# A two-layer hybrid decoder on one core: other layouts for the stored queries and keys, a norm vector moved into weights, and reordered work at the stage borders

## Chip, core and metric

The kernel runs on one core of a Trainium2 chip. The metric is the device time of one execution in microseconds (us). TensorE multiplies matrices and also does the transposes; VectorE (DVE), ScalarE (ACT) and GpSimd (POOL) work on tiles; SyncE (SP) issues nearly all DMAs here, and 16 DMA engines carry them out.

## The reference, cut to what matters

```python
D_MODEL, SEQ, DEPTH = 1024, 1024, 2       # 8 heads of 64 of either kind, 32 experts of width 256
def rms_norm(x, gain):
    return x * rsqrt(mean(x * x, -1) + 1e-6) * gain

def hybrid_mixer(xn, ...):                # xn = rms_norm(h, attn_norm[l])
    fq, fk, fv, f_logit, c_q, c_kv, k_rope = split(xn @ w_in)
    fox = attention(fq, fk, fv, decay=cumsum(log_sigmoid(f_logit + b_f)))
    q  = rms_norm(c_q, q_norm) @ w_uq     # 64 plain + 32 rotary columns per head
    kv = rms_norm(c_kv, kv_norm) @ w_ukv  # 64 key + 64 value columns per head
    mla = attention(rotary(q), [k_nope, rotary(k_rope)], v)
    return concat(norm(fox), norm(mla)) @ w_o

def reference(x, ...):
    h = x
    for l in range(DEPTH):
        h = h + hybrid_mixer(rms_norm(h, attn_norm[l]), ...)
        h = h + hierarchical_moe(rms_norm(h, ffn_norm[l]), ...)   # top 1 group, top 2 experts in it
    return rms_norm(h, final_norm)
```

All inputs and the output are float32.

## The kernel before, in words

Every product is made of split operands: `split` (L181 to L188) writes a rounded high part on ScalarE (L184, L187) and the rest on DVE (L185, L188), and `mm3` (L190 to L196) makes three TensorE passes of them. `split` takes a scale per partition if one is given.

A layer runs through these stages, each written out as straight code for 8 blocks of 128 tokens:

1. *Norm and first projection* (`chain_a`, `chain_b`, `transposes`, `misc_mm`, L405 to L486). For each block: in layer 1 the two expert rows y are added to h (`chain_c`); ScalarE squares and sums (L412); GpSimd takes the rsqrt in six small steps (`mean_rsqrt`, `rsqrt`, L163 to L179); DVE multiplies the row by its rsqrt and by the vector `attn_norm`, which a DMA has spread over all 128 partitions (`gb`, L417); TensorE transposes the block in eight pieces (L426), whose copies are split into xT; and `misc_mm` multiplies it with the 424 columns of w_in that hold the forget logits and the latents. The weights of these columns come in 8 pieces (`wa_piece`). In the loop at L475 block i+1 is transposed ahead of the projection of block i.
2. *Projections* (L745 to L797). Six chunks of 256 columns of w_in: v twice, (q, 0), (q, 1), (k, 0), (k, 1). The weights of the next chunk are loaded and split while a chunk runs (`prepare`: per chunk four pieces of two row blocks, 512 columns in all). A q or k chunk has four steps, each with one product of 24 passes; `take` splits the result into a staging tile `st` and stores it in HBM: FQ holds per head the high part twice and the low part once, FK the low and the high part, and both hold four more rows per head for ones and for the decay (`forget_d`). Each step then runs a few jobs of a list: first 18 jobs for decay, latents and rotary keys, then 12 for V, and from `late_pools` on (at (k, 0)) loads of w_uq and w_ukv and the upward projections: rotary and plain queries (MQR, MQ) and plain keys (MK).
3. *Hand-over* (L799 to L839). `load_ops` reads the four operand tiles of head 0 back from FQ and FK, the last FK result is taken, 8 value products follow, and `load_ops` of head 1. The operand buffers `op` lie where the second half of xT was.
4. *Attention*, 16 heads with two operand buffers (`load_ops` again, one head ahead), and the output projection with the router.
5. *Experts*, 32 per layer; the weights stream in. A loop for crowded experts follows (L1614), which ran no round in the profiled execution.

Behind the second layer the last stage (L1648 to L1668) adds the two expert rows to each block (`combined`, L225), takes the norm and stores the block; the output of a block is made behind the next block's sum.

TensorE, ScalarE, DVE and GpSimd execute in the order written. The order of SP's DMAs is chosen by a planner when the kernel is built: among the DMAs that its model holds to be ready, the one written first. Each engine runs its queue in order, so an instruction that waits holds up all behind it.

## Time and profile before

| | |
|---|---|
| median of 3 runs | 1942.1 us (1937.24 to 1949.56) |
| the profiled execution: time, span | 1941.36 us, 1939.6 us |
| TensorE busy, mean granted clock | 90% of the span, 0.959 |
| DVE, ScalarE, GpSimd busy | 70%, 61%, 30% |
| HBM read, written | 347.24 MB, 94.37 MB |
| layer 0: norm and first projection, projections, attention and output, experts | about 0 to 60, 60 to 238, 238 to 620, 620 to 932 us |
| layer 1, the same | about 932 to 1010, 1010 to 1182, 1182 to 1560, 1560 to 1875 us |
| last stage | 1875 to 1939.6 us |

Shares are of the span of one profiled execution. The granted clock is TensorE's: 1.0 is 2.4 GHz, 0.5 is 1.2 GHz. A busy engine need not be the bound, and an idle one costs only where the work that ends last waits for it.

### The profile page before, as it was taken

The numbers are of one execution on the slowest core, as the hardware profiler recorded it, in microseconds if no ns is written. First come the engines' busy times: TensorE is split into PE (matmuls) and PEld (weight loads), VectorE is DVE, ScalarE is ACT, GpSimd is POOL, SyncE is SP. The second block draws the span as 40 slices with busy tenths as digits, with TensorE's granted clock in tenths as the row PEclk, the third lists the DMA queues.
The fourth block names the chain that finished last, engine by engine and source line by source line (L and its number), as shares of the span: only waits on it lengthen the run. The fifth ranks groups of instructions, "written<-read, shape, count | busy, mean of one in ns | idle before, by whom it ended". The sixth has DMA issues, their size and how long they took to land.

```text
span 1939.6 us, 33742 instructions
## 1 busy us (share of the span) xinstructions
PE 1742.0 (90%) x12509; PEld 1410.5 (73%) x12509; DVE 1362.6 (70%) x2180; ACT 1184.9 (61%) x2254; POOL 587.2 (30%) x849
## 2 busy tenths in 40 slices
PE   7999899999996999999499997999999979999960
PEld 6987678888785777666399876888878757776640
DVE  6463478888336999888565345888863689998855
ACT  4442378888312898878344334888861268888751
POOL 4001145233313334332331021532241243343315
PEclk9999989999997999999799998999999979999995
DMA  5247833453763999999742776344547479999986
GB/s 162 66 114 213 274 134 111 101 121 88 248 210 135 359 357 353 362 353 357 273 156 53 185 242 219 110 121 107 119 144 251 153 268 365 350 347 358 351 298 221
DMA packets 145380, 427.11 MB, mean 220 GB/s; under 512 B 22166, under 2 KB 37564, under 8 KB 142140
## 3 DMA queue, kind: packets, MB, share of 16 engines
q1 hardware_dynamic: 129788, 387.14, 60.5%
q0 software_dynamic: 14336, 33.58, 5.2%
q10 hardware_dynamic: 1088, 4.19, 0.6%
q8 instruction: 100, 1.64, 0.4%
q14 instruction: 68, 0.56, 0.1%
HBM read 347.24 MB, written 94.37 MB: 228 GB/s over the span
## 4 chain that ended last, share of the span: by engine, by line
PE 60%; DMA 24%; DVE 6%; ACT 6%; issue 2%; POOL 1%; SPq 1%; POOLq 0%; ACTq 0%; DVEq 0%
PE ps L194 9%; PE ps L195 9%; PE ps L196 9%; DMA gu<-in_w_gate_dram 8%; PE S L873 8%; DMA gu<-in_w_up_dram 6%; PE pt L902 6%; DMA dn<-in_w_down_dram 6%; PE y L916 3%; PE gu L195 2%; PE gu L196 2%; PE gu L194 2%; ACT pr L894 2%; PE y L1140 1%; DVE nm L885 1%
## 5 line engine op out<-in xcount | busy, mean ns | idle before, releaser
L1482 DVE TENSOR_TENSOR lo<-gu,hi 128x1024 fp32r<-128x1024 f32 x248 | 298.0, 1221 | 42.1 <-ACT hi L1481 41.3
L1481 ACT ACTIVATE hi<-gu 128x1024 fp32r<-128x1024 f32 x248 | 257.9, 1059 | 29.7 <-DMA gu<-in_w_up_dram 21.1
L873 PE MATMUL S<-op 96*128 96x512 f32 (+3 forms) x960 | 228.8, 372 | 18.2 <-DMA op<-FK 11.6
L885 DVE TENSOR_REDUCE nm<-S 128x1 f32<-128x1024 f32 (+7 forms) x256 | 183.1, 752 | 67.2 <-PE S L877 67.2
L195 PE MATMUL gu<-lo,V 128*96 128x512 f32 x512 | 206.0, 402 | 11.9 <-DVE lo L1482 11.5
L894 ACT ACTIVATE pr<-S,nm 128x1024 f32<-128x1024 f32 (+7 forms) x256 | 189.2, 755 | 36.3 <-DVE nm L885 36.1
L194 PE MATMUL gu<-hi,V 128*96 128x512 f32 x512 | 206.8, 404 | 1.2 <-ACT hi L1481 0.6
L196 PE MATMUL gu<-hi,V 128*96 128x512 f32 x512 | 204.0, 399 | 0.9 <-DVE V L185 0.3
L904 ACT ACTIVATE ph<-pt 128x512 f16<-128x512 f32 x288 | 157.3, 601 | 66.6 <-PE pt L902 65.7
L1531 POOL DMA_INDIRECT y<-V,sidx x64 | 81.9, 1280 | 372.8 <-ACT V L1530 359.2
L905 DVE SCALAR_TENSOR_TENSOR pl<-pt,ph 128x512 f16<-128x512 f32 x288 | 184.7, 682 | 8.9 <-ACT ph L904 7.8
L873 PEld LDWEIGHTS S<-op 96*128 96x128 f32 (+1 forms) x960 | 161.3, 196 | 35.7 <-DMA wor<-in_w_o_dram 6.9
L1482 DVE TENSOR_TENSOR lo<-dn,hi 128x1024 fp32r<-128x1024 f32 x128 | 156.1, 1221 | 18.4 <-ACT hi L1481 14.8
L902 PE MATMUL pt<-ident,pr 128*128 128x128 f32 x1152 | 155.2, 278 | 8.6 <-DVE pl L905 3.5
L1481 ACT ACTIVATE hi<-dn 128x1024 fp32r<-128x1024 f32 x128 | 135.0, 1056 | 21.5 <-DMA dn<-in_w_down_dram 21.3
L902 PEld LDWEIGHTS pt<-ident,pr 128*128 128x128 f32 x1152 | 125.4, 143 | 13.9 <-ACT pr L894 13.0
L195 PEld LDWEIGHTS gu<-lo,V 128*96 128x96 f32 x512 | 83.5, 163 | 58.6 <-DVE lo L1482 29.0
L916 PE MATMUL y<-V,ph 128*128 128x64 f16 x2304 | 121.6, 193 | 2.8 <-ACT ph L904 1.6
L916 PEld LDWEIGHTS <-ph 128*128 128x128 f16 x2304 | 116.9, 98 | 5.3 <-ACT ph L904 1.8
L916 PE MATMUL y<-V,pl 128*128 128x64 f16 x1152 | 117.0, 193 | 1.1 <-DVE pl L905 1.0
L196 PEld LDWEIGHTS gu<-hi,V 128*96 128x96 f32 x512 | 83.4, 163 | 38.3 <-DVE V L185 6.2
L175 POOL TENSOR_SCALAR rs_v<-ss 128x1 f32<-128x1 f32 (+1 forms) x44 | 20.6, 468 | 289.6 <-ACT xn L1096 150.5
(363 smaller groups left out, 4366.0 us busy)
## 6 DMA issues: line engine op xcount, KB each, us to landing
gu<-in_w_gate_dram SPq DMA_DIRECT2D x124, 512.0 KB
gu<-in_w_up_dram SPq DMA_DIRECT2D x124, 512.0 KB
dn<-in_w_down_dram SPq DMA_DIRECT2D x60, 1024.0 KB
raw<-in_w_in_dram SPq DMA_DIRECT2D x48, 256.0 KB
h<-ht SPq DMA_DIRECT2D x17, 512.0 KB
FQ<-st SPq DMA_DIRECT2D x32, 256.0 KB
FK<-st SPq DMA_DIRECT2D x32, 256.0 KB
MQ<-st SPq DMA_DIRECT2D x16, 512.0 KB
```

The costliest lines, as they stand in the source:

```text
L194: pe.matmul(ps, sh(kc), mh(kc), start=first and i == 0, stop=False)
L195: pe.matmul(ps, sh(kc), ml(kc), start=False, stop=False)
L196: pe.matmul(ps, sl(kc), mh(kc), start=False, stop=last and i == n - 1)
L873: pe.matmul(o, a[0:k, qs], b[0:k, c0:c0 + n], start=bank not in started, stop=pi == len(passes) - 1 and not diag, skip_group_check=True)
L885: dve.tensor_reduce(nm, u["S"][:, col:col + (qb + 1) * P], axis=AX.X, op=OP.max, negate=True)
L894: act.activation(u["pr"][:, s], u["S"][:, s], AF.Exp, bias=nm, accum_out=zst[h // 2][:, qb, h % 2:h % 2 + 1])
L902: pe.transpose(pt[:, b], u["pr"][:, (4 * q + b) * P:(4 * q + b + 1) * P], ident)
L904: act.activation(u["ph"][:, ks], pt, AF.Copy, scale=P_SCALE)
L905: dve.scalar_tensor_tensor(u["pl"][:, ks], pt, P_SCALE, u["ph"][:, ks], op0=OP.mult, op1=OP.subtract)
L916: pe.matmul(yst[h][:, qb], a[:, b], v[:, kb, h % H, c], start=first_y[h], stop=(kb == qb and s == 2), skip_group_check=True)
L1481: act.activation(h_, raw, AF.Copy)
L1482: eng.tensor_tensor(l_, raw, h_.bitcast(F32), op=OP.subtract)
```

## The change

- FQ and FK are stored in the layout [head x 64 rows, 2 parts, tokens], with the rows for ones and decay in small tensors of their own (FQC, FKC). A result of 128 rows (two heads) goes out in one DMA. `load_ops` reads six pieces in place of four: each part into partitions 0 to 63, the part that is needed twice a second time into partitions 64 to 127, and the four extra rows.
- `late_pools` stands one chunk earlier, at (q, 1); every step runs 3 jobs (4 before in the k chunks). Four of the eight MK products are taken out of the list and made between the first four value products of the hand-over, behind the loads of head 0.
- `attn_norm` is no longer spread over the partitions. Its 16 rows are loaded once, transposed on TensorE into the columns `ga`, and the splits of the w_in pieces take their column as scale. Pieces of two row blocks are therefore split in two halves of 256 columns. The rows of h are scaled on ScalarE.
- The first projection stands in front of the transposes of block 1; its copy out of PSUM (`misc_take`) stands where it was.
- The block h[7] is loaded into a second staging tile; the tile `ht` is gone.
- Last stage: the sixteen y loads get sixteen tiles and are written ahead of the load of `final_norm`; the output of a block is made behind the sum of the block after next.

The diff, without the lines that only hand over a parameter or a tile:

```diff
+    arow = const.tile([DEPTH * KC, P], F32, name="arow")
+    sp.dma_start(arow, attn_norm.rearrange("l (c p) -> (l c) p", p=P))
+    ga = const.tile([P, DEPTH * KC], F32, name="ga")
...
-        gb = stg.tile([P, D], F32, name="st")
-        hx.append(stg.tile([P, D], F32, name="st"))
+        hx += [stg.tile([P, D], F32, name="st") for _ in range(2)]
...
-                    bcast_row(gb, attn_norm[l])
...
-        FQ = dram.tile([H, 3 * HD + 4, T], F32R, name=f"FQ{l}")
-        FK = dram.tile([H, 2 * HD + 4, T], F32R, name=f"FK{l}")
+        FQ = dram.tile([H * HD, 2, T], F32R, name=f"FQ{l}")
+        FK = dram.tile([H * HD, 2, T], F32R, name=f"FK{l}")
+        FQC = dram.tile([H, 4, T], F32R, name=f"FQC{l}")
+        FKC = dram.tile([H, 4, T], F32R, name=f"FKC{l}")
...
-            split(wah[k], wal[k], wraw[k])
+            split(wah[k], wal[k], wraw[k], ga[:, l * KC + k:l * KC + k + 1])
...
-            dve.scalar_tensor_tensor(xn, ht, rstd, gb, op0=OP.mult, op1=OP.mult)
+            act.activation(xn, ht, AF.Copy, scale=rstd)
...
-            h_load(NT - 1)
         else:
             h_load(0)
+            pg = pp.tile([P, 512], F32, name="ps")
+            pe.transpose(pg[:, 0:DEPTH * KC], arow, ident[:DEPTH * KC, :DEPTH * KC])
+            dve.tensor_copy(ga, pg[:, 0:DEPTH * KC])
             chain_a(0)
             wa_piece(0)
             wa_piece(1)
-            bcast_row(gb, attn_norm[l])
...
+            if i == 0:
+                misc_mm(i)
             if i + 1 < NT:
                 transposes(i + 1)
             if i + 3 < NT:
                 chain_a(i + 3)
             if i + 2 < NT:
                 chain_b(i + 2)
-            misc_mm(i)
+            if i:
+                misc_mm(i)
+            misc_take(i)
...
-                split(hi, lo, rs[j])
+                for q in range(2):
+                    k, qs = l * KC + 2 * j + q, slice(q * 256, q * 256 + 256)
+                    split(hi[:, qs], lo[:, qs], rs[j][:, qs], ga[:, k:k + 1])
...
-            jobs.extend(kj)
+            jobs.extend(kj[:4])
+            late["kj"] = kj[4:]
...
-            if (nm, half) == ("k", 0):
+            if (nm, half) == ("q", 1):
                 late_pools()
...
-                        for e in range(2):
-                            h, rs = 2 * j + e, slice(e * HD, (e + 1) * HD)
-                            if nm == "q":
-                                move(FQ[h, HD:3 * HD].rearrange("(b r) t -> r b t", r=HD)[:, :, cs], st[rs])
-                                move(FQ[h, 0:HD, cs], st[rs, 0])
-                            else:
-                                move(FK[h, 0:2 * HD].rearrange("(b r) t -> r b t", r=HD)[:, :, cs], st[rs])
+                        move((FQ if nm == "q" else FK)[j * P:(j + 1) * P, :, cs], st)
...
-                    run(jobs, 4 if nm == "k" else 3)
+                    run(jobs, 3)
...
-                move(o[:, 0], FQ[h, 0:2 * HD])
-                move(o[:, 2], FK[h, 0:2 * HD])
-                move(o[0:HD + 4, 1], FQ[h, 2 * HD:])
-                move(o[0:HD + 4, 3], FK[h, HD:])
+                hs = slice(h * HD, (h + 1) * HD)
+                move(o[0:HD, 0:2], FQ[hs])
+                move(o[HD:, 0], FQ[hs, 0])
+                move(o[0:HD, 2:4], FK[hs])
+                move(o[HD:, 2], FK[hs, 1])
+                move(o[HD:HD + 4, 1], FQC[h])
+                move(o[HD:HD + 4, 3], FKC[h])
...
         opnd = {0: load_ops(0)}
         take()
+        run(jobs, len(jobs))
...
             v_take(vraw2[:, i], ps, NT + i)
-        run(jobs, len(jobs))
+            if i < len(late["kj"]):
+                late["kj"][i]()
         opnd[1] = load_ops(1)
...
     gb = cb.tile([P, D], F32, name="gb")
+    ys = [[cb.tile([P, D], F32, name="y", bufs=2 * NT) for _ in range(2)] for _ in range(NT)]
+    for i in range(NT):
+        for j in range(2):
+            sp.dma_start(ys[i][j], y_d[DEPTH - 1][j * T + i * P:j * T + (i + 1) * P])
     bcast_row(gb, final_norm)
...
-    for i in range(NT + 1):
+    for i in range(NT + 2):
         if i < NT:
             last_a(i)
-        if i:
-            ht, ot, rstd = st[i - 1]
-            dve.scalar_tensor_tensor(ot, ht, rstd, gb, op0=OP.mult, op1=OP.mult)
-            sp.dma_start(out[0, (i - 1) * P:i * P], ot)
+        if i > 1:
+            last_b(i - 2)
```

## Rows read from the trace of the kernel before

Rows of windows give the stretch in us, its length, then busy us (and instructions) of PE, PEld, DVE, ACT and POOL, the granted clock, the DMA share and GB/s. Rows of the timeline give the start, the busy time (both us), the engine, line, operation, output<-inputs and shapes, a count, and in brackets the idle time before it and what ended that. SPq is SP's queue: the time there is that of issuing.

**Rows 1.** Windows by stage: hand-over in layer 0, experts of layer 1.
```profile
225.00:250.00 25.00, 15.32 (x61) 11.59 (x60) 9.32 (x15) 7.52 (x14) 0.00 (x0) 0.81 0.85 271
...
1560.00:1875.00 315.00, 300.90 (x1463) 209.89 (x1464) 274.37 (x335) 259.02 (x383) 115.15 (x94) 0.98 0.97 345
```

**Rows 2.** Timeline of the hand-overs of both layers, TensorE and DVE.
```profile
233.06 4.27 DVE L628 TENSOR_REDUCE mx<-ps 128x1 f32<-128x512 f32 x7
...
235.01 0.39 PE L196 MATMUL ps<-uk,ck 128*128 128x512 f32 x1
238.24 0.47 PE L873 MATMUL S<-op 128*128 128x512 f32 x1 [2.84 <-DMA op<-FK]
245.29 1.62 PE L873 MATMUL S<-op 68*128 68x512 f32 x3 [6.58 <-DMA wor<-in_w_o_dram]
...
1182.33 0.55 PE L873 MATMUL S<-op 128*128 128x512 f32 x1 [2.81 <-DMA op<-FK]
...
1188.88 1.62 PE L873 MATMUL S<-op 68*128 68x512 f32 x3 [6.00 <-DMA op<-FK]
```

**Rows 3.** Timeline of SP's DMA queue in the projections of layer 0.
```profile
152.76 12.13 SPq L93 DMA_DIRECT2D FQ<-st  x12
164.93 1.68 SPq L686 DMA_DIRECT2D raw<-in_w_uq_dram  x2
...
225.07 5.44 SPq L93 DMA_DIRECT2D MK<-st  x4
230.61 0.65 SPq L93 DMA_DIRECT2D op<-FQ  x1
```

**Rows 4.** Windows behind the two hand-overs.
```profile
245.30:254.00 8.70, 8.44 (x31) 6.75 (x32) 4.29 (x7) 3.74 (x8) 0.00 (x0) 0.50 0.42 147
1188.90:1197.00 8.10, 7.84 (x30) 6.07 (x31) 4.10 (x7) 3.62 (x8) 0.00 (x0) 0.55 0.44 157
```

**Rows 5.** Windows with one kind of transfer: FQ stores, MK stores, two operand loads.
```profile
154.00:156.00 2.00, 2.00 (x11) 1.65 (x10) 0.00 (x0) 0.52 (x2) 0.00 (x0) 1.00 0.99 196
220.00:222.00 2.00, 2.00 (x11) 1.63 (x10) 0.69 (x1) 0.40 (x1) 0.00 (x0) 1.00 1.05 399
274.00:277.00 3.00, 3.00 (x46) 2.59 (x42) 2.74 (x4) 2.74 (x8) 2.73 (x5) 1.00 0.83 324
376.00:383.00 7.00, 6.60 (x84) 5.75 (x82) 6.14 (x10) 5.66 (x13) 0.47 (x2) 1.00 0.95 218
```

**Rows 6.** Timeline of operand loads in attention, layer 0, and a first use.
```profile
260.26 0.33 SPq L93 DMA_DIRECT2D op<-FQ  x1
...
274.04 1.19 PE L873 MATMUL S<-op 128*128 128x512 f32 x4
...
374.94 0.45 SPq L93 DMA_DIRECT2D op<-MQ  x1
```

**Rows 7.** Windows in the projections of layer 0 and layer 1.
```profile
172.00:178.00 6.00, 3.95 (x14) 2.08 (x14) 1.39 (x2) 1.26 (x2) 0.00 (x0) 1.00 0.60 184
1100.00:1150.00 50.00, 48.86 (x213) 39.58 (x212) 21.43 (x39) 17.21 (x32) 7.62 (x6) 1.00 0.76 232
```

**Rows 8.** Timeline of the norm stages, layer 0 and layer 1.
```profile
9.20 1.28 DVE L417 SCALAR_TENSOR_TENSOR xn<-cq,rs_d,st 128x1024 f32<-128x1024 f32 x1 [1.23 <-DMA st<-in_attn_norm_dram]
...
970.52 1.62 PE L426 MATMUL ps<-ident,xn 128*128 128x128 f32 x8 [3.28 <-DVE xn L417]
```

**Rows 9.** Timeline of the last stage.
```profile
1882.99 0.34 SPq L199 DMA_DIRECT2D gb<-in_final_norm_dram  x1
...
1901.84 1.47 POOL L166 TENSOR_TENSOR rs_y<-rs_v,mhalf 128x1 f32<-128x1 f32 x1
...
1928.20 1.28 DVE L1665 SCALAR_TENSOR_TENSOR ot<-gu,rs_d,gb 128x1024 f32<-128x1024 f32 x1 [1.82 <-POOL rs_d L171]
```

**Rows 10.** Window of the y loads in the last stage.
```profile
1883.00:1896.00 13.00, 0.00 (x0) 0.00 (x0) 5.35 (x5) 2.30 (x4) 2.63 (x7) 0.50 0.86 323
```

**Rows 11.** Timeline of SP's queue in the norm stage of layer 0.
```profile
27.84 0.36 SPq L93 DMA_DIRECT2D FQ<-trix  x1
```

More of the change, by code (lines that the diff above doesn't have):

```diff
@@ L160, with rsqrt, mean_rsqrt @@
     more = const.tile([P, NX + 1], I32, name="more")
-    def rsqrt(dst, v, n, tag, c=1.0):
+    def rsqrt(dst, v, n, tag, c=1.0, eng=pool):
         y = small.tile([P, n], F32, name="rs_y", tag=f"rs_y{tag}")
-        pool.tensor_tensor(y, v, mhalf[:, 0:n], op=OP.pow)
+        eng.tensor_tensor(y, v, mhalf[:, 0:n], op=OP.pow)
         t = small.tile([P, n], F32, name="rs_t", tag=f"rs_t{tag}")
-        pool.tensor_tensor(t, y, y, op=OP.mult)
-        pool.tensor_tensor(t, t, v, op=OP.mult)
-        pool.tensor_scalar(t, t, -0.5 * c, 1.5 * c, op0=OP.mult, op1=OP.add)
-        pool.tensor_tensor(dst, y, t, op=OP.mult)
-    def mean_rsqrt(ss, scale, n, tag, d=None):
+        eng.tensor_tensor(t, y, y, op=OP.mult)
+        eng.tensor_tensor(t, t, v, op=OP.mult)
+        eng.tensor_scalar(t, t, -0.5 * c, 1.5 * c, op0=OP.mult, op1=OP.add)
+        eng.tensor_tensor(dst, y, t, op=OP.mult)
+    def mean_rsqrt(ss, scale, n, tag, d=None, eng=pool):
         v = small.tile([P, n], F32, name="rs_v", tag=f"rs_v{tag}")
-        pool.tensor_scalar(v, ss, scale, EPS, op0=OP.mult, op1=OP.add)
+        eng.tensor_scalar(v, ss, scale, EPS, op0=OP.mult, op1=OP.add)
         if d is None:
             d = small.tile([P, n], F32, name="rs_d", tag=f"rs_d{tag}")
-        rsqrt(d, v, n, tag)
+        rsqrt(d, v, n, tag, eng=eng)
         return d
@@ L362, in mixer_open @@
                         wraw[k] = wa_load(raws, l, k)
-                    bcast_row(gb, attn_norm[l])
-        return lat, lat_close, stg, stg_close, raws, raws_close, hx, gb, wraw
+        return lat, lat_close, stg, stg_close, raws, raws_close, hx, wraw
     def mixer(l, opened):
@@ L381, in mixer @@
         xT = [xp.tile([P, KC, T], F32R, name=f"xT{s}") for s in range(2)]
-        lat, lat_close, stg, stg_close, raws, raws_close, hx, gb, wraw = opened
+        lat, lat_close, stg, stg_close, raws, raws_close, hx, wraw = opened
         mi, mi_close = open_pool(f"misc{l}", "right")
@@ L395, in wa_piece @@
                 wraw[k] = wa_load(raws, l, k)
-            split(wah[k], wal[k], wraw[k])
+            split(wah[k], wal[k], wraw[k], ga[:, l * KC + k:l * KC + k + 1])
         xs = {}
-        hx.append(nrm.tile([P, D], F32, name="ht"))
         def h_load(i):
@@ L412, in chain_a @@
             act.activation(xn, ht, AF.Square, accum_out=ss)
-            xs[i] = (ht, mean_rsqrt(ss, 1.0 / D, 1, "1"), xn)
+            xs[i] = (ht, mean_rsqrt(ss, 1.0 / D, 1, "1", eng=pool), xn)
         def chain_b(i):
             ht, rstd, xn = xs[i]
-            dve.scalar_tensor_tensor(xn, ht, rstd, gb, op0=OP.mult, op1=OP.mult)
+            act.activation(xn, ht, AF.Copy, scale=rstd)
             xs[i] = xn
@@ L427, in transposes @@
                 split(xT[0][:, 4 * q:4 * q + 4, ts], xT[1][:, 4 * q:4 * q + 4, ts], pt)
+        mps = {}
         def misc_mm(i):
-            ps = pp.tile([P, 512], F32, name="ps")
+            ps = mps[i] = pp.tile([P, 512], F32, name="ps")
             ts = slice(i * P, (i + 1) * P)
@@ L433, in misc_mm, with misc_take @@
                 range(KC))
-            act.activation(misc[:, i], ps[:, :MISC], AF.Copy)
+        def misc_take(i):
+            act.activation(misc[:, i], mps[i][:, :MISC], AF.Copy)
         tjobs, jobs = deque(), deque()
@@ L570, in forget_d @@
             cs = slice(c * 512, c * 512 + 512)
-            for dst, sgn in ((FQ[:, 3 * HD + 2:, cs], None), (FK[:, 2 * HD:2 * HD + 2, cs], -1.0)):
+            for dst, sgn in ((FQC[:, 2:, cs], None), (FKC[:, 0:2, cs], -1.0)):
                 st = stg.tile([P, 2, 512], F32R, name="st")[0:H]
@@ L660, in mixer @@
         one = trix[0:H, None, P:].to_broadcast([H, 16, P])
-        for dst in (FQ[:, 3 * HD:3 * HD + 2], FK[:, 2 * HD + 2:]):
+        for dst in (FQC[:, 0:2], FKC[:, 2:]):
             move(dst.rearrange("h r (c t) -> h (r c) t", t=P), one)
@@ L1653, in last_a @@
     def last_a(i):
-        ht = combined(DEPTH, i, got[0][i], lambda j: cb.tile([P, D], F32, name="y", bufs=8))
+        ht = got[0][i]
+        for j in range(2):
+            dve.scalar_tensor_tensor(ht, ys[i][j], gates[:, j, i:i + 1], ht, op0=OP.mult, op1=OP.add)
         ot = cb.tile([P, D], F32, name="ot", bufs=4)
@@ L1658, in last_a, with last_b @@
         st[i] = ht, ot, mean_rsqrt(ss, 1.0 / D, 1, "1")
-    for i in range(NT + 1):
+    def last_b(i):
+        ht, ot, rstd = st[i]
+        dve.scalar_tensor_tensor(ot, ht, rstd, gb, op0=OP.mult, op1=OP.mult)
+        sp.dma_start(out[0, i * P:(i + 1) * P], ot)
+    for i in range(NT + 2):
         if i < NT:
             last_a(i)
-        if i:
-            ht, ot, rstd = st[i - 1]
-            dve.scalar_tensor_tensor(ot, ht, rstd, gb, op0=OP.mult, op1=OP.mult)
-            sp.dma_start(out[0, (i - 1) * P:i * P], ot)
+        if i > 1:
+            last_b(i - 2)
     cb_close()
```

## The prediction

> **What bounds the kernel now.** I read the windows by stage first. In both projection stages and both attentions TensorE is busy nearly all the time; the expert stages run at a DMA share of 0.97 [rows 1]. The change touches none of the matmul work and nothing in the expert loop, so its worth lies in the places of those stages, and at the ends, where TensorE stands idle: the hand-over from projections to attention (15.32 of 25 us busy in layer 0), a hole in the projections, and the 65 us after the last expert, where TensorE has nothing to do.
>
> The timeline of TensorE at the hand-over is read next [rows 2]. The last projection matmul starts at 235.01 and takes 0.39. The first score pass comes after 2.84 idle, the next one after 6.58 more: 9.42 us in which the operands of head 0 are missing. Layer 1 repeats it: 2.81 + 6.00 = 8.81. The issue rows of SP say why [rows 3]: the loads of head 0 are issued at 230.61, right behind four MK stores (225.07, 5.44 us), into a busy queue. Before that SP needs 12.13 us for twelve FQ stores, and only behind them, at 164.93, are the w_uq loads issued. After the idle time TensorE runs at the lower clock of its two levels (granted 0.50) for 8.7 us in layer 0 and nearly so (0.55) for 8.1 us in layer 1 [rows 4].
>
> **The change, part by part.** Terms are set against the profiled execution: span 1939.6, its own time 1941.4, which is 0.7 under the median of the three runs.
>
> *Stores and job order.* Each layer's 32 FQ and FK stores of 64 partitions, and 16 more with FQ's duplicate rows, become 16 stores of 128 partitions. FQ stores ran at 196 GB/s with the engines 0.99 busy, the 128-partition MK stores at 399 [rows 5]; and 2 MB per layer are no longer written. The upward projections begin one chunk earlier, in (q, 1), where before no job was left: the first 18 jobs end within the two v chunks, the 12 of V within (q, 0). (k, 1) then carries no job, and four of the eight MK jobs move behind the loads of head 0, between the value rows. Total TensorE work is the same; what moves is who stands before the loads on SP: FK stores alone, one per 5.5 us.
>
> When are head 0's operands there? Their buffer lies on the second half of xT, so the loads can't start before the last use of it, in the last FK product, whose end is the start of the value rows, 8 x 3 passes of 0.23 before 235.40, so about 229.9 in layer 0. Behind it TensorE still has 8 value rows and now 4 MK products, 12 x 3 passes x 0.23 = 8.3 us. The loads change form, from two of 128 partitions and two of 68 to 64-partition halves. The row nearest to that is an MLA head's load, 64 and 32 partitions: 218 GB/s at a share of 0.95, against 324 for the old form [rows 5]; its 1.57 MB, issued at 374.94 [rows 6], are in by about 383.2, so 8.2 us. 8.2 against 8.3: it just fits, with some slack since DVE needs 2 us more: its last maximum ended at 233.06 + 4.27 = 237.33 [rows 2], 1.9 behind TensorE's 235.40, and score banks are freed by it. So idle time falls from 9.42 to about 2.0 and from 8.81 to 1.9: -7.4 and -6.9. Bounds: 0 (loads still late) to -9.4 and -8.8.
>
> By the Trainium skill (DMA: Bandwidth & Descriptors, Rules for kernel authors) two transfers to the two partition halves should not be made, since they serialize on the same engines; one 128-partition transfer is better. That speaks against this load; by it the 1.57 MB come some 2.4 us later than in the old form (218 against 324 GB/s), and if none of that were hidden the sum would be 5 us worse in the two layers. The trace agrees on the rate and bears on the hiding only through the 8.3 us above.
>
> *Clock.* In the half-clock stretches TensorE was busy 8.44 and 7.84 us; at full clock that is at most -4.2 and -3.9 [rows 4]. But the ramp is a chain of scores, row maximum, exponential and transposes, not TensorE alone, and 2 us of idle time stay. I take -2.5 and -2.0; bounds 0 and the halves.
>
> *The hole in the projections.* TensorE waits 2.04 us at 172 to 178 and 1.1 us in 1100 to 1150 for w_uq [rows 7]. Twelve FQ stores stand before these loads on SP [rows 3]; now one store per step does. -2.0 and -1.1, bounds 0 and the same.
>
> *Norm vector into the weights.* The broadcast of 512 KB is gone, as is DVE's 1.28 per token block; ScalarE takes 1.06 instead. It was late once: DVE waited 1.23 for it at 9.20 [rows 8]. Row scaling comes free with the split's scale operand; the 24 splits of 512 columns per layer become 48 of 256 (about 0.36 for 0.62 on ScalarE), under a TensorE that is full; only the first chunk shows, +0.3 per layer. The new order starts the first projection some 3 us earlier, but all of TensorE's queue behind it moves: the second transposes now follow the projection, then ScalarE makes their two copies (1.09), the square of block 3 (1.24) and only then the scaling of block 2 (1.06) that the third transposes wait for. Projection 0 to projection 1 is thus 0.5 + 1.1 + 1.2 + 1.1 + 0.9 = about 5 us, of which TensorE works 2. The head start is spent: projection 1 comes at about 25.2 again. In layer 1 the same chain exists already (3.28 idle at 970.52 [rows 8]); my walk through its queues ends at 971.9 against 972.1. What is new is a 3 us hole in layer 0, and a stretch at the lower clock may follow it, as it follows the 9 us at the hand-over: +1.0 in all with the splits, bounds -3 and +4.
>
> *The end.* All sixteen y loads are issued first, the final norm vector behind them. Before, it was first (1882.99) [rows 9]. 323 GB/s flowed from 1883 to 1896 [rows 10], the expert stage holds 345 [rows 1]; 17 x 0.524 MB = 8.9 MB from 1883.0 lands by about 1908. DVE's queue is block 0, block 1, block 2, output 0, block 3, ...; output 0 needs that vector. So DVE does three blocks by 1897 and stops until 1908; block 3 stands behind it. From there: five pairs (2.6 each) and eight outputs (1.28) make 23.2 us of DVE alone; GpSimd's rsqrt, 0.19 per step when DVE rests but up to 1.47 beside it [rows 9], adds about 5 in waits. The last output ends at 1936.3 instead of 1929.5 [rows 9]: +6.8; bounds +2 (no GpSimd wait) and +9. The second block of lag helps only the steady pace, about 4.7 us per block, which is set by DVE's 3.9 plus what GpSimd can't do beside it.
>
> *The sum.* -7.4 - 6.9 - 2.5 - 2.0 - 2.0 - 1.1 + 1.0 + 6.8 = -14.1: 1927.3 on this execution, 1928 on the scale of the median.
>
> **The rivals.** (1) *The vector is not behind the y loads.* SP's order is the planner's, not the text's: layer 1's constant rows of FQ were stored at 27.84, a whole layer early, and in the text that is behind the first loop [rows 11]. If it takes the vector first, DVE runs on: output 0 at 1897.5, then 4.7 per block, last output at 1927.7. The end gives -1.8 instead of +6.8: 1919. Against it: behind the loop all these loads become ready together, and the rows after the first loop (y before the next blocks' work) follow the text. (2) *Operands still late.* Loads in halves plus one more store at the wrong place, and half of the idle time stays (4 us per layer) with its clock loss: 1928 + 6.5 + 6.0 = 1940. For it: 8.2 against 8.3 leaves nothing; against it: the DMA queue is nearly empty in the last chunk, and DVE gives 2 us more. (3) *Slower: the halves bind in every forgetting head.* The load of head 2 is issued at 260.26 and first used at 274.04, so it may take 13.8 us [rows 6]. Beyond that each of the twelve later forgetting heads of the two layers waits, and from about 15.0 us (12 x 1.2 = 14) the whole change loses; at 16 us it is 12 x 2.2 = 26: 1954. The MLA rows at 8.2 us with the same slack and no wait speak against it.
>
> **How the numbers follow.** Chances: forecast 0.46 (1923 to 1934), rival 1 0.25 (1914 to 1923), rival 2 0.16, rival 3 0.05, the rest (both ends better than bounded, or a loss in the norm stage) 0.08. From 1914 to 1939 lie the first two and half of rival 2. A change of 1%, about what a measurement can tell here, is 19.4 us: under 1922.7 falls most of rival 1 and little of the forecast, 0.32; over 1961.5 0.04; between 0.64.
>
> **What would show it.** In the profile after: score idle of about 2 us at the hand-over and a granted clock near 1.00 behind it; no TensorE wait on w_uq; FQ stores at the rate of MK's; a TensorE hole of 3 us between the first two projections of layer 0; DVE idle some 11 us in the end stage, released by the final norm vector. The forecast is wrong if SP issues that vector first, if the operands land after the value rows, or if the clock falls in the 2 us that remain.

## The result, and the profile after

The changed kernel takes 1931.55 us (median of 9 runs, 1927.46 to 1935.2), the kernel before 1942.1 beside it: ratio 0.9941, 95% interval 0.9924 to 0.9958. That lies in the range, 3.5 us above the forecast of 1928.0, and the change is under 1%, to which the prediction gave a chance of 0.64. The sum came out nearly right by luck: two of its terms were far off, and they cancel. One of the five executions of best1 below took 2520.35 us at a mean granted clock of 0.646; it is left out, and best1's time is the median of the other four.

The profiled execution took 1934.76 us, span 1933.0 (before 1941.36 and 1939.6): 6.6 us less, where the medians say 10.6; the nine executions lie within 8 us. Two later runs (gb_last and tail below) have the same code up to the last stage, so their profiles show how far one stage scatters. Each value is the distance between two points on TensorE's timeline: the start of the span, the end of the last projection matmul, the first transposes of the experts, and so on.

| stretch, us | before | changed kernel | the same code in gb_last, tail | mean change | forecast |
|---|---|---|---|---|---|
| start to last projection matmul, layer 0 | 235.40 | 232.61 | 234.43, 233.59 | -1.9 | -2.0 (hole) and the norm |
| from there to the experts' first transposes | 388.76 | 384.32 | 382.77, 385.14 | -4.7 | -9.9 (hand-over, clock) |
| experts, layer 0, to layer 1's first transposes | 330.56 | 329.88 | 328.96, 330.67 | -0.7 | 0 |
| layer 1, to the last projection matmul | 224.79 | 226.93 | 224.84, 224.81 | +0.7 | -1.1 (hole) and the norm |
| from there to the experts' first transposes | 386.15 | 385.51 | 384.42, 383.18 | -1.8 | -8.9 (hand-over, clock) |
| experts, layer 1, to the last matmul | 311.40 | 312.62 | 313.36, 312.50 | +1.4 | 0 |
| last stage | 62.54 | 61.13 | (changed there) | -1.4 | +6.8 |

The norm term of the forecast, +1.0, belongs to both layers. The row of the hand-over is where most of the forecast gain is missing, and the last stage is where the forecast loss is missing.

The hand-over first: the timeline of SP, ScalarE, DVE and TensorE in the changed kernel, layer 0 and then layer 1.

```profile
224.22 1.15 SPq L93 DMA_DIRECT2D op<-FQ  x2
...
227.60 0.56 SPq L93 DMA_DIRECT2D FK<-st  x1
228.26 9.29 SPq L93 DMA_DIRECT2D MK<-st  x4
235.69 0.60 ACT L188 ACTIVATE st<-ps 128x512 fp32r<-128x512 f32 x1 [5.85 <-DMA FK<-st]
236.18 2.06 ACT L640 ACTIVATE vraw<-ps 128x512 f32<-128x512 f32 x4
236.93 2.48 DVE L641 TENSOR_REDUCE mx<-ps 128x1 f32<-128x512 f32 x4
238.26 2.08 PE L887 MATMUL S<-op 128*128 128x512 f32 x4 [5.66 <-DVE mx L641]
...
1176.61 0.60 ACT L188 ACTIVATE st<-ps 128x512 fp32r<-128x512 f32 x1 [5.63 <-DMA FK<-st]
1180.37 2.08 PE L887 MATMUL S<-op 128*128 128x512 f32 x4 [6.63 <-DVE mx L641]
```

Against [rows 2, 3]: the loads of head 0 are issued 6.4 us earlier, ahead of the MK stores, as the forecast had it, and the idle time falls from 9.42 and 8.81 to 5.66 and 6.63. But what ends it is no longer a load. Read the rows upwards: TensorE waits for DVE's maxima, these for ScalarE's copies, and the copies stand behind one split of an MK product that waited 5.85 us for an FK store to finish reading its staging tile. That store is issued at 227.60, behind six loads.

Behind it the clock is low again. These are windows of layer 0 from the first score on; columns as in [rows 4], the clock is the last but two (layer 1: 0.58 as the mean of its first 10 us):

```profile
238.26:242.26 4.00, 4.00 (x12) 2.79 (x12) 2.37 (x3) 0.49 (x1) 0.00 (x0) 0.50 1.03 285
242.26:246.26 4.00, 3.74 (x17) 3.27 (x16) 2.58 (x4) 2.54 (x5) 0.00 (x0) 0.50 1.00 223
```

The norm stages: timeline of TensorE and ScalarE, the third transposes of layer 0 and the waits in layer 1.

```profile
23.32 1.09 PE L428 MATMUL ps<-ident,xn 128*128 128x128 f32 x8 [2.81 <-ACT xn L419]
...
955.34 1.06 ACT L414 ACTIVATE xn<-cq 128x1024 f32<-128x1024 f32 x1 [3.28 <-DVE cq L229]
956.39 1.17 ACT L191 ACTIVATE wah<-raw,ga 128x424 fp32r<-128x424 f32 x2
957.08 0.72 PE L198 MATMUL ps<-wah,xT 128*128 128x424 f32 x1 [3.57 <-ACT wah L191]
...
964.38 1.97 PE L428 MATMUL ps<-ident,xn 128*128 128x128 f32 x8 [2.76 <-ACT xn L419]
```

The 2.81 is the 3 us hole that was forecast for layer 0. The 3.57 was not: the first projection of layer 1 now starts before the last weight halves are split, and those stand on ScalarE behind the square of block 2, which waits for its own block. The w_uq waits of [rows 7], 2.04 and 1.1 us, are 0.97 (at 151.34) and 0.38 (at 1093.15). A window behind an FQ store that was issued at 127.11 with no other transfer beside it, columns as in [rows 5]:

```profile
128.00:130.00 2.00, 2.00 (x10) 1.68 (x9) 1.21 (x3) 1.92 (x4) 0.00 (x0) 1.00 0.70 262
```

262 GB/s at a share of 0.70 would be about 374 at a full share (196 at 0.99 before, MK's 399 at 1.05 [rows 5]): FQ stores now run at about the rate of MK's, as the prediction has it.

The last stage: timeline of SP, DVE and GpSimd.

```profile
1877.56 0.33 SPq L203 DMA_DIRECT2D gb<-in_final_norm_dram  x1
1877.94 14.80 SPq L1667 DMA_DIRECT2D y<-y  x16
...
1896.57 1.28 DVE L1682 SCALAR_TENSOR_TENSOR ot<-gu,rs_d,gb 128x1024 f32<-128x1024 f32 x1 [0.90 <-POOL rs_d L175]
1896.62 1.28 POOL L179 TENSOR_SCALAR rs_v<-ss 128x1 f32<-128x1 f32 x1
1897.99 1.47 POOL L170 TENSOR_TENSOR rs_y<-rs_v,mhalf 128x1 f32<-128x1 f32 x1
1899.54 0.89 POOL L172 TENSOR_TENSOR rs_t<-rs_y 128x1 f32<-128x1 f32 x1
1900.51 0.19 POOL L173 TENSOR_TENSOR rs_t<-rs_t,rs_v 128x1 f32<-128x1 f32 x1
...
1901.28 1.28 DVE L1682 SCALAR_TENSOR_TENSOR ot<-gu,rs_d,gb 128x1024 f32<-128x1024 f32 x1 [0.90 <-POOL rs_d L175]
```

SP issues the final norm vector first, as before [rows 9], though in the text it stands behind the y loads: rival 1. The outputs then come every 4.71 us, each released by GpSimd's chain of six small steps.

### The profile page after: what moved, and what is told of

Read it like the earlier page. It is cut to its first block, busy times and chain, and to the rows that moved or that the text cites. A ratio compares the mean times of both kernels' runs of the same rounds, so it can differ in the third digit from the quotient of the medians.

```text
span 1933.0 us, 33752 instructions
## 1 busy us (share of the span) xinstructions
PE 1746.2 (90%) x12510; PEld 1413.1 (73%) x12510; DVE 1363.6 (71%) x2213; ACT 1215.9 (63%) x2318; POOL 581.4 (30%) x849
```

## The experiments

### Who holds the score banks

Theory: the staging tile under the late FK store. Rivals: the loads of head 0 themselves; DVE's own work. **stage** gives the four late MK products four tiles of their own:

```
         ops, ops_close = open_pool(f"ops{l}", "left", 2)
+        lst, lst_close = open_pool(f"lst{l}", "left", 4)
+        late["st"] = lst
...
-                st = stage()
+                st = late["st"].tile([P, 2, 512], F32R, name="st") if "st" in late else stage()
...
         opnd[1] = load_ops(1)
+        lst_close()
```

> The changed kernel, but the four late MK products are staged in four tiles of their own, so that none waits for a tile from which an FK store is still being read. Theory (that tile is what holds ScalarE, and with it the copies, the maxima and the score banks): the idle time in front of the first score pass falls from 5.65 us (layer 0) and 6.63 us (layer 1) to 1 to 2.5 us each, ScalarE shows no wait on FK<-st there, and the time falls 6 to 12 us below the changed kernel's 1931.5, to 1920 to 1926, the more the shorter the half-clock stretch behind it becomes. Rival 1 (head 0's loads are themselves not in before about 238): the wait goes over to the loads, idle 4 to 6 us, time within 2 us of 1931.5. Rival 2 (DVE's maxima are late by their own work): idle unchanged with ScalarE free.

Measured: 1930.95, ratio 0.9925 (0.9907 to 0.9944). Timeline of TensorE and ScalarE:

```profile
236.14 0.47 PE L890 MATMUL S<-op 128*128 128x512 f32 x1 [1.24 <-DMA op<-FK]
...
243.13 1.11 ACT L911 ACTIVATE pr<-S,nm 128x1024 f32<-128x1024 f32 x1 [7.60 <-DMA MK<-st]
244.39 1.97 PE L919 MATMUL pt<-ident,pr 128*128 128x128 f32 x8 [5.16 <-ACT pr L911]
```

The idle time in front of the first scores is 1.24 (layer 1: 1.48), as the theory has it, and as mechanisms both rivals fall. But the time hardly moved and missed the theory's 1920 to 1926: the new tiles lie where the attention puts its first exponentials, and these now wait 7.60 us for the MK stores. The wait was moved, not removed, and this run says nothing yet of its price. **stage_cos** puts two of the products where nothing is needed soon, in the memory of the position tables:

```
-            cosT = upw.tile([P, T], F32, name="cosT")
-            sinT = upw.tile([P, T], F32, name="sinT")
+            cosT = upw.tile([P, T], F32, name="cosT", tag="own0")
+            sinT = upw.tile([P, T], F32, name="sinT", tag="own1")
...
-                st = stage()
+                st = upw.tile([P, 2, 512], F32R, name="st", tag=own) if own else stage()
```

(`own` is set for the last two MK products alone.)

> The changed kernel; the last two of the four late MK products are staged in the memory of the two position tables, which are no longer needed by then, instead of in the rotating tiles. Nothing else differs: the instructions of TensorE, DVE, ScalarE and GpSimd are the same, and the attention's first tiles don't lie on it (they did in the run with four tiles of their own, where the idle time in front of the first scores fell to 1.2 us and the row maxima and exponentials then waited up to 7.6 us for the MK stores). Theory (staging tile held by the FK store): idle in front of the first scores about 1.2 to 2.5 us in each layer, no ScalarE wait on FK<-st and none on MK<-st, so the gain stays: 7 to 10 us less than the changed kernel, ratio to the kernel before about 0.989 to 0.991. Rival (the gain always goes to the next wait, here the loads of head 0 or head 1): ratio 0.993 to 0.995, as in the changed kernel.

Measured: 1924.45, ratio 0.9901 (0.9878 to 0.9925). First a window, then TensorE's timeline:

```profile
235.27:239.27 4.00, 2.71 (x13) 1.73 (x13) 2.35 (x3) 1.11 (x2) 0.00 (x0) 1.00 1.06 407
```
```profile
235.27 1.52 PE L887 MATMUL S<-op 128*128 128x512 f32 x4 [1.45 <-DVE mx L641]
...
250.76 0.99 PE L887 MATMUL S<-op 128*128 128x512 f32 x2 [1.94 <-DMA op<-FK]
```

1.45 us idle in layer 0, 1.41 in layer 1, and a clock of 1.00 for the first 10 us behind it in both: here are the forecast's 2 us and its clock. The first transposes of probabilities come 5.6 us behind the last projection matmul instead of 10.4. Some of it is given back: a later head's operands, issued at 235.20, are 1.94 us late at 250.76. From the last projection matmul to the experts it is 380.92 and 381.25 us, 3.2 and 3.1 less than the means of the table, and less than each of the three profiles behind them.

**fk_first** keeps the tiles and moves the store; **mk_back** takes the MK products away from there:

```
-        opnd = {0: load_ops(0)}
-        take()
+        take()
+        opnd = {0: load_ops(0)}
```

> The changed kernel with one thing changed, the order on SP: the last FK store is issued behind the first load of head 0 instead of behind its sixth. Theory (staging tile): the store lands some 3 us earlier, ScalarE's fourth MK split with it, and the idle time falls from 5.65 and 6.63 to 2 to 4 us, the time by 3 to 8 us to 1924 to 1929. Rival (loads late): the loads come a store (1.3 us) later, idle 6 to 8 us, the time rises by 1 to 4 us.

```
-            jobs.extend(kj[:4])
-            late["kj"] = kj[4:]
+            jobs.extend(kj)
+            late["kj"] = []
```

> The changed kernel, but all eight MK products stay in the last two projection chunks, so that no MK store stands behind the loads of head 0 and none of the products covers them. Theory (staging tile): no split waits for the FK store, but only 8 value rows (5.5 us of TensorE) are left behind the point where the loads may start; with 8 to 9 us for the loads the idle time is about 3 us, released by the loads, 1.0 to 3 us less than in the changed kernel in each layer; 1926 to 1931. Rival (the move of the four MK products is what shortened the gap): idle 8 to 9 us as in the kernel before, time back by 5 to 7 us, 1936 to 1939.

Measured: fk_first 1923.2, ratio 0.9889 (0.9868 to 0.991); mk_back 1926.69, ratio 0.9911 (0.989 to 0.9931). First scores, fk_first and then mk_back:

```profile
227.05 0.52 SPq L93 DMA_DIRECT2D FK<-st  x1
232.12 0.60 ACT L188 ACTIVATE st<-ps 128x512 fp32r<-128x512 f32 x1 [1.04 <-DMA FK<-st]
237.07 0.47 PE L887 MATMUL S<-op 128*128 128x512 f32 x1 [3.23 <-issue]
```
```profile
238.26 0.47 PE L887 MATMUL S<-op 128*128 128x512 f32 x1 [4.37 <-DMA op<-FK]
```

With one load in front of the store instead of six, ScalarE's wait falls from 5.85 to 1.04 us and the idle time to 3.23 (layer 1: 2.84), now set by the loads (layer 1 names them; in layer 0 the next pass waits for one). The theory holds a third time. From the last projection matmul to the experts it is 380.14 and 378.89 us, 3.9 and 5.5 less than the means, more than stage_cos gained with half the idle time; why is not shown. The granted clock over the 10 us from the first score on is 0.66 in layer 0, but 1.00 in layer 1, behind 2.84 us of idle time. In mk_back nothing waits for the staging tile either, and the loads, issued at 228.22, end the wait 10.0 us later. From the first transposes of a layer to its experts mk_back takes 605.45 and 606.99 us, 3.0 and 2.9 less than the means of the changed kernel's three profiles and less than each of them (its ratio alone, with overlapping intervals, would not settle it). So the rival that the move of the four products was itself the gain falls: with the tile held, the move cost more than its cover was worth.

### The layout

**layout_old** is the changed kernel with the old FQ and FK: 64-partition stores with the duplicate rows, loads of 128 and 68 partitions:

```
-                        move((FQ if nm == "q" else FK)[j * P:(j + 1) * P, :, cs], st)
+                        for e in range(2):
+                            h, rs = 2 * j + e, slice(e * HD, (e + 1) * HD)
+                            if nm == "q":
+                                move(FQ[h, HD:3 * HD].rearrange("(b r) t -> r b t", r=HD)[:, :, cs], st[rs])
+                                move(FQ[h, 0:HD, cs], st[rs, 0])
...
```

> The changed kernel with the old form of the forgetting heads' operands: stores in 64-partition halves with FQ's duplicate rows (12 and 8 per chunk instead of 4), loads of head 0 to 7 as two of 128 and two of 68 partitions. It prices the layout. Theory (as in the forecast: fewer and wider stores clear the w_uq hole, the half-partition loads cost little because they are hidden): DMA share in the query chunks back to about 0.8, and the time 1 to 5 us above the changed kernel, ratio 0.995 to 0.997. Rival 1 (the half-partition loads bind at the hand-over, about 2.4 us a layer): the old loads are in earlier and the ratio falls to 0.990 to 0.993. Rival 2 (the gap at the hand-over grows, since twice the FK stores stand in front of the loads): idle over 8 us in each layer, ratio 0.998 to 1.001.

Measured: 1946.85, ratio 1.002 (1.0002 to 1.0039): no faster than the kernel before, and above the ranges of the theory and of both rivals. Timeline of TensorE, SP and ScalarE:

```profile
156.01 0.50 PE L198 MATMUL ps<-cq,uq 128*128 128x512 f32 x1 [4.42 <-ACT uq L188]
...
216.22 11.55 SPq L93 DMA_DIRECT2D FK<-st  x6
...
243.53 0.60 ACT L188 ACTIVATE st<-ps 128x512 fp32r<-128x512 f32 x1 [7.51 <-DMA FK<-st]
246.10 2.07 PE L888 MATMUL S<-op 128*128 128x512 f32 x4 [7.31 <-DVE mx L639]
...
1105.03 0.50 PE L198 MATMUL ps<-cq,uq 128*128 128x512 f32 x1 [2.77 <-ACT uq L188]
```

The w_uq waits are 4.42 and 2.8 us, more than before, because the upward projections now begin a chunk earlier and the weights are still behind stores. The projections take 4.9 us (layer 0) and 3.4 us (layer 1) more than the means of the table, hand-over and attention 2.2 and 1.9 more: 12.4 of the 15 us. In form this is nearest to rival 2: six FK stores are issued one behind the other (11.55 us), the same ScalarE wait for a staging tile is 7.51 us instead of 5.85, and the idle time in front of the scores 7.31, short of the 8 that the rival has. So in this job order the new layout is worth far more than the 3.1 us of the hole: without it the earlier projections wait for their weights. The run puts back stores and loads at once, so it does not price them apart.

### The norm stage

**order** puts the first projection behind the second transposes again, **scale_dve** scales the rows on DVE:

```
-            if i == 0:
-                misc_mm(i)
...
-            if i:
-                misc_mm(i)
+            misc_mm(i)
             misc_take(i)
```

> The changed kernel with the first projection of each layer behind the second block's transposes again. By the forecast's walk through the queues the head start of this order is spent by the second projection, so that the time hardly changes: the hole of 2.8 us between the two projections of layer 0 goes, the first projection of layer 0 comes some 3 us later, and the last projection matmul of layer 0 ends within 1.5 us of 232.6 counted from the same start; ratio 0.993 to 0.996. Rival (the head start is a gain, the third block's transposes don't wait for more than before): 2 to 3 us lost per layer, ratio 0.996 to 0.998.

```
-            act.activation(xn, ht, AF.Copy, scale=rstd)
+            dve.tensor_scalar(xn, ht, rstd, None, op0=OP.mult)
```

> The changed kernel with the rows of the token blocks scaled on DVE again (norm vector still in the weights). Theory (ScalarE, in order, is what the norm stage waits for): TensorE's 3.6 us wait for a weight half in layer 1 and its waits on the scaled rows fall by 3 to 6 us in the two layers together, ratio 0.991 to 0.993. Rival (DVE has as much to do there, so the wait only changes its name): the waits of TensorE in the two norm stages keep their sum within 1.5 us, ratio 0.993 to 0.996.

Measured: order 1924.21, ratio 0.9899 (0.987 to 0.9928); scale_dve 1926.49, ratio 0.9916 (0.9887 to 0.9945). The order's ratio is lower than both expectations, and its last projection matmul of layer 0 ends at 231.13, 1.5 us ahead of 232.6: the old order looks better (the two intervals of the ratio still overlap, by 0.0004). TensorE's passes of the first projection show why, the changed kernel first, then order:

```profile
11.84 0.72 PE L198 MATMUL ps<-wah,xT 128*128 128x424 f32 x1 [0.81 <-ACT xT L188]
...
17.41 0.56 PE L198 MATMUL ps<-wah,xT 128*128 128x424 f32 x1
17.76 0.52 PE L199 MATMUL ps<-wal,xT 128*128 128x424 f32 x1
18.11 0.36 PE L200 MATMUL ps<-wah,xT 128*128 128x424 f32 x1
```
```profile
17.20 0.56 PE L198 MATMUL ps<-wah,xT 128*128 128x424 f32 x1
17.55 0.49 PE L199 MATMUL ps<-wal,xT 128*128 128x424 f32 x1
17.88 0.35 PE L200 MATMUL ps<-wah,xT 128*128 128x424 f32 x1
...
22.33 0.44 PE L198 MATMUL ps<-wah,xT 128*128 128x424 f32 x1
```

Passes start every 0.35 us until about 18 in both kernels, and every 0.19 from there. The new order starts the projection 4.1 us earlier (11.84 against 15.99), spends 17 of its 24 passes at the slow pace instead of 5, and is 2.1 us ahead at its end. Then comes the hole of 2.81, and the second projection starts at 24.16 where order has it at 22.33. In the six other profiles with the same norm stage and the same TensorE work up to the last projection matmul (gb_last, tail, stage, stage_cos, fk_first, mk_back) the slow passes are 9 to 16, the hole is 2.81 every time, and the second projection starts at 23.84 to 24.82. Over the whole projection stage of layer 0, order is 2.7 us shorter than the mean of the changed kernel (221.64 against 224.4 from the first transposes on), and outside the 223.55 to 225.65 of all seven; in layer 1 it is 0.9 shorter, which is inside the scatter. Its hand-over and attention in layer 1 are also 3.2 us shorter. There ScalarE waits 5.27 us for the FK store as before, but the first score passes wait only 1.22 and the next ones 3.65, 4.87 us in all instead of 6.63. Why the first score bank is free earlier there is not shown.

With DVE scaling, TensorE's waits in layer 1 are 2.7 (weight half) and 2.1 us (rows) instead of 3.6 and 2.8, and in layer 0 the hole is 2.23: 2.2 us less idle in all, less than the theory's 3 to 6. Its projection stage of layer 1 is 2.7 us shorter (222.87 against 225.5), that of layer 0 0.7 (inside the scatter). The times alone don't separate this kernel from the changed one.

### The last stage

**gb_last** makes the forecast's mistake true, **tail** takes GpSimd's steps away except for the power:

```
+    sp.dma_start(gb[:, 0:1], ys[6][0][:, 0:1])
     bcast_row(gb, final_norm)
```

> The changed kernel with the final norm vector forced behind the y loads (one 128x1 copy out of the thirteenth y tile into the vector's tile stands in front of its load). It prices the step of the forecast that did not come true. By the forecast's reckoning DVE stops for about 11 us at the first output until the vector is in (some 25 to 28 us after the first y load), and the last output comes 6 to 9 us later than in the changed kernel: 1937 to 1941. Rival (the stage is set by GpSimd's rsqrt at 4.7 us per block, which goes on while DVE waits): the stop is partly made up, +2 to +4 us: 1933 to 1936.

```
-        st[i] = ht, ot, mean_rsqrt(ss, 1.0 / D, 1, "1")
+        act.activation(v, ss, AF.Copy, scale=1.0 / D, bias=EPS)
+        pool.tensor_tensor(y, v, mhalf[:, 0:1], op=OP.pow)
+        st[i] = ht, ot, v, y
...
+        dve.tensor_tensor(t, y, y, op=OP.mult)
+        dve.tensor_tensor(t, t, v, op=OP.mult)
+        dve.tensor_scalar(t, t, -0.5, 1.5, op0=OP.mult, op1=OP.add)
+        dve.tensor_tensor(rstd, y, t, op=OP.mult)
         dve.scalar_tensor_tensor(ot, ht, rstd, gb, op0=OP.mult, op1=OP.mult)
```

> The changed kernel with the last stage's reciprocal square roots taken from GpSimd except for the power itself: scale and offset on ScalarE behind the square, the four refining steps on DVE in front of the output they serve, two blocks later. Theory (the end is set by GpSimd's chain, some 4.7 us per block, in which its steps take 0.2 to 1.5 us each because DVE works beside them): the chain falls to DVE's own 4.1 us per block, the last output comes 3 to 6 us earlier behind the last matmul (61.1 us in the changed kernel's profile, 56 to 58 here), ratio 0.991 to 0.993. Rival (DVE is the bound, or the y loads): the four steps lengthen DVE's queue by 0.3 us per block and the end stays within 1.5 us or comes 1 to 3 us later.

Measured: gb_last 1943.15, ratio 0.9997 (0.9985 to 1.001); tail 1927.89, ratio 0.9924 (0.9898 to 0.9949). DVE's timeline in gb_last, then DVE's and GpSimd's groups of tail from the y loads on (busy us and mean ns; idle us in front and its releasers):

```profile
1901.68 1.29 DVE L1683 SCALAR_TENSOR_TENSOR ot<-gu,rs_d,gb 128x1024 f32<-128x1024 f32 x1 [15.40 <-DMA gb<-in_final_norm_dram]
```
```profile
L1692 DVE SCALAR_TENSOR_TENSOR ot<-gu,rs_d,gb 128x1024 f32<-128x1024 f32 x8 | 10.3, 1285 | 0.3
...
L1681 POOL TENSOR_TENSOR rs_y<-rs_v,mhalf 128x1 f32<-128x1 f32 x8 | 9.4, 1173 | 33.1 <-ACT rs_v L1679 19.5 <-DMA y<-y 13.6
```

A vector behind the y loads stops DVE for 15.4 us and makes the last stage 10.1 us longer (71.22 against 61.13), the time 0.56% or 10.9 us. Against the kernel before the stage is 8.7 us longer, where the forecast had +6.8 with a bound of +9. The forecast's mechanism is right and its price somewhat low; its condition did not hold. The rival, which has the stop partly made up, falls. In tail the outputs wait 0.3 us in all for anything, and the stage is 5.0 us shorter (56.11): GpSimd's chain was the bound. The time's own interval overlaps that of the changed kernel.

### The corrections together

**best1** joins stage_cos, order and scale_dve; **best2** has fk_first in place of stage_cos; **all_four** is best1 with tail. They hold no new code.

> Three corrections of the changed kernel at once: the last two late MK products staged in the memory of the position tables, rows scaled on DVE, first projection behind the second transposes. If they are independent: minus 7.7 us (hand-over), 4 to 5 (scaling) and 2 to 5 (order; the lower bound by its projection stage alone), so 1931.5 - 14 to 18, about 1914 to 1918, ratio 0.985 to 0.988. If scaling and order mend the same wait: ratio 0.987 to 0.989. The half-clock stretch behind the hand-over stays away (granted 1.00 in the first 10 us of scores).

> As the run with three corrections, but at the hand-over the last FK store is issued behind the first load of head 0 in place of the other staging memory. The wait for the loads of head 0 (about 3 us in each layer, behind which the clock fell to 0.50) stays, and the next heads' loads are not late. By the two single runs (ratio 0.9889 and 0.9901) it comes within 0.3% of the other combination: 0.984 to 0.988. If the clock's fall is the larger price it is 2 to 4 us slower than the other; if the late loads of the third head are, 2 to 4 us faster.

> The three corrections together with the last stage's steps taken from GpSimd. The last stage lies apart from the others, so its 5.0 us (61.13 to 56.11 us behind the last matmul in the profiles) should add in full to the ratio 0.9875 of the three: 0.984 to 0.986, about 1911 to 1915 where the kernel before takes 1942. If the last stage's gain in the single run was only its expert stage's scatter from run to run, the ratio stays at 0.987 to 0.989.

Measured: best1 1916.5, ratio 0.9875 (0.9851 to 0.9898); best2 1917.88, ratio 0.9875 (0.9852 to 0.9897); all_four 1911.12, ratio 0.9845 (0.9825 to 0.9865), 1.55% under the kernel before and the fastest here. In best1 the stretches of the table are 229.87, 378.66 and 222.70, 379.54. Its ratio lies in the ranges of both expectations, so it does not say whether scaling and order mend the same wait. The stretches say that they mostly add: from the first transposes on, best1's projection stages are 3.6 and 2.8 us shorter than the means, where order alone gave 2.7 and 0.9 and scaling alone 0.7 and 2.7, that is 3.4 and 3.6. The last stage adds in full (all_four is 5.0 us shorter than best1 there). best1 and best2 can't be told apart, and the price of a half-clock stretch against that of a late load stays open: best2 starts its scores at a low clock (0.57, then 0.50, in layer 0), but best1 does so too in layer 1, behind 1.28 us of idle time. That part of its expectation (1.00 in the first 10 us of scores) held in layer 0 alone:

```profile
1161.21:1171.21 10.00, 8.51 (x37) 6.86 (x37) 5.60 (x10) 4.63 (x10) 0.00 (x0) 0.66 1.07 329
```

## Why the prediction was right, point by point

The time is right, the mechanism only in part. Of the prediction's own signs, the FQ stores at MK's rate and the hole of 3 us in layer 0 came. But all three things came too by which it calls itself wrong: SP issued the vector first, the clock fell behind the hand-over, and the operands land behind the value rows (this shows once the staging tile is out of the way: in stage the first score waits 1.24 us for them).

- **Hand-over: the step that failed** is "DVE needs 2 us more: its last maximum ended ... 1.9 behind TensorE's". The loads went ahead of the MK stores as said, but so did they go ahead of the last FK store, and the fourth of the moved MK products needs the tile that this store reads. The maximum ended some 6.8 us behind TensorE (239.41 against 232.61). Forecast -14.3 for idle time in both layers, measured -3.8 and -2.2. Shown by stage, stage_cos and fk_first. **Rival 2** came true in its size (half of the idle time and the clock loss stay) and in naming one more store in the wrong place, but not in its mechanism: it has the operands late, and the wait was for a tile behind them. Late operands were the next wait, 1 to 4 us, in stage, fk_first and mk_back, where the tile no longer holds.
- **Clock.** -2.5 and -2.0 did not come: 5.7 and 6.6 us of idle time stayed, and the clock was at 0.50 behind it. With 1.45 and 1.41 us, in stage_cos, it stayed at 1.00, but a short wait does not settle it: it fell behind 1.28 us in layer 1 of best1 and stayed behind 2.84 us in layer 1 of fk_first.
- **Loads of head 0.** 8.2 us was too low: 10.0 us from issue to first score in mk_back, with a store beside them. It was too low in its own row already: behind the window that was read, the engines are still busy from 383 to 384 us at a share of 0.35, so about 9 us. By the Trainium skill (DMA: Bandwidth & Descriptors, Rules for kernel authors) two half-partition transfers serialize, and one of 128 partitions is better. The trace agrees that the halves take more time of the DMA engines (DMA shares of 0.65, 0.99, 0.82 and 0.00 in the four stretches of 3 us behind such an issue at 279.69, against 0.65, 0.50, 0.28 and 0.09 in the old form at 286.52 before: about 7.4 us of all 16 engines against 4.6), but not that they come later: with nothing beside it, a head's load in attention ended sooner in the new form (last section). The prediction's 2.4 us more for the new form is in no run, and the old loads with the old stores made the kernel 15 us slower (layout_old).
- **Hole in the projections.** 0.97 and 0.38 us stayed, so -1.1 and -0.7 for -2.0 and -1.1. Right in kind. Behind it the forecast missed what the layout carries: without it the earlier projections wait 7.2 us (layout_old).
- **Norm.** The walk for layer 0 was right (hole of 3 us: 2.81; second projection at about 25.2: 24.16). What it didn't see is that the alternative was better by 2 to 3 us in layer 0, and that in layer 1 weight halves come late (3.57). Its +1.0 lies near the +0.7 that the table leaves without the hole, but the same code scatters by 2 us there.
- **The end: wrong step**, "All sixteen y loads are issued first, the final norm vector behind them": SP issued the vector at 1877.56, ahead of them, and DVE's wait at the first output is 0.63 us instead of some 11. **Rival 1** came true, -1.4 for its -1.8. The step time of 0.19 us that the prediction sets against 1.47 belongs to the plain steps; 1.47 is the power, which takes 0.55 alone (last section).
- **Rival 3** (half loads bind in every forgetting head) did not occur: in the changed kernel no score pass waits for operands.

Rival 1's end (8.6 below the forecast's) on rival 2's time of 1940 gives 1931.4; measured 1931.55. The forecast's own sum was near by luck: it took the gain of the hand-over 12 us too high (-18.8 with the clock, measured -6.5 as the table's mean) and that of the end 8.2 us too low (+6.8, measured -1.4).

## What to carry to other kernels

When a store is moved behind loads in a queue, follow its source tile: whoever is to refill that tile waits for the whole stretch of loads in front, and everything behind him in his engine's queue waits with him. A tile added to break such a wait must not lie where the next stage writes first (stage, 7.60 us). And where a term hangs on the order of a queue that a planner sets, forecast both orders, since the text doesn't say which it will be.

## What the runs showed of the hardware that was not expected

- The first projection's passes came every 0.35 us at first and every 0.19 from about 18 us on. The windows 12 to 16 and 16 to 20 give a granted clock of 1.00 there, but that is no reading: the first clock record of the trace stands at 18.10 us (order: 17.83), just where the pace doubles, and a window counts time without a record as 1.00. Twice the time per pass is what the lower of the two levels would give. In the changed kernel TensorE had run one block's transposes and 17 passes before the pace rose, in order two blocks of transposes and 5 passes. A head start at the slow pace is worth half of what it looks like: 4.1 us at the first pass, 2.1 at the last.
- The length of an idle stretch alone doesn't tell whether the clock falls. The same code with the same hole of 2.81 us in the first norm stage stands in eight profiles: in the changed kernel's the clock stayed at 1.00 behind it, in the seven others (gb_last, tail, stage, stage_cos, fk_first, mk_back, layout_old) it fell to 0.50 within 1.3 us of the hole's end. The same stretch in the changed kernel and in gb_last:

```profile
24.50:28.00 3.50, 3.50 (x20) 3.43 (x19) 1.29 (x2) 2.67 (x5) 2.88 (x13) 1.00 0.78 238
24.50:28.00 3.50, 3.50 (x12) 3.26 (x11) 1.29 (x2) 2.68 (x5) 2.88 (x13) 0.51 0.77 242
```

- A forgetting head's load in 64-partition halves keeps the DMA engines busier than the old form and still ends sooner, where nothing else is transferred. The first row is the kernel before, the end of the MLA load from which the prediction took its 8.2 us. The second is the kernel before, 9 to 11 us behind the first issue (286.52) of a forgetting head's load, which still moves data; the third is the changed kernel, 9 to 11 us behind such an issue (279.69), with the engines silent:

```profile
383.00:384.00 1.00, 1.00 (x12) 0.97 (x11) 0.45 (x2) 0.52 (x2) 0.00 (x0) 1.00 0.35 74
295.52:297.52 2.00, 1.80 (x24) 1.44 (x20) 2.00 (x5) 1.02 (x3) 0.00 (x0) 1.00 0.14 51
288.69:290.69 2.00, 1.80 (x24) 1.43 (x20) 2.00 (x5) 1.02 (x3) 0.00 (x0) 1.00 0.00 0
```

- In the last stage GpSimd's plain steps on 128x1 take 0.19 us and the power 0.55 when DVE rests; beside DVE's 1.28 us operations they take up to 1.29 and 1.47. By the Trainium skill (SBUF — State Buffer, Who interferes with whom) a DVE instruction with two SBUF inputs contends with a GpSimd one that reads SBUF, and the port pair that they share is an exclusive lock. The trace agrees: the steps that start beside a DVE operation last until its end or shortly behind it, and taking all but the power off GpSimd made the stage 5.0 us shorter.
